# Modulation tiles loaded ahead of their use, eight scaled tiles per boundary, and head sums as single float32 products

## The chip, the cores and the metric

The kernel runs on one core of a Trainium2 chip. The time is device microseconds (us) of one execution. Three executions of the kernel before took 2766.11, 2750.26 and 2754.33 us; the time before is their median, 2754.33 us.

## What is computed

One sequence of 256 tokens with 2048 channels goes through two layers, all in float32. The first layer mixes time by an RWKV-7 recurrence (32 heads of 64 channels), the second by attention over chunks of 64 tokens that reads one shared pair of keys and values. Each has a squared-ReLU MLP of 8192 hidden channels behind it. Ahead of every block the residual stream is normed and modulated, and its gate comes from the same modulation. Cut to what the change touches:

```python
def rms_norm(x, g):
    return x * rsqrt(mean(x * x, axis=-1) + RMS_EPS) * g
def modulate(h, shift, scale):
    return h * (1 + scale) + shift

for layer in range(2):
    sh1, sc1, gt1, sh2, sc2, gt2 = split(c @ w_ada[layer] + b_ada[layer], 6)
    if layer == 1:
        sh_kv, sc_kv = split(c @ w_ada_kv + b_ada_kv, 2)
        h_kv = modulate(rms_norm(x, g_kv), sh_kv, sc_kv)
        kp, vp = h_kv @ w_k_shared, h_kv @ w_v_shared
    h = modulate(rms_norm(x, g_mix[layer]), sh1, sc1)
    y = rwkv7_time_mix(h, ...) if layer == 0 else chunk_band_attention(h, kp, vp, ...)
    x = x + gt1 * y                     # y ends in a 2048x2048 product, "out projection"
    h = modulate(rms_norm(x, g_mlp[layer]), sh2, sc2)
    x = x + gt2 * (square(relu(h @ w_up[layer])) @ w_down[layer])
return rms_norm(x, g_final)

# inside rwkv7_time_mix, per head: three sums over the head's 64 channels
kk = kk / max(sqrt(sum(kk * kk)), 1e-12)
y = (y - mean) * rsqrt(mean((y - mean)**2) + GN_EPS) * ln_w + ln_b
y = y + sum(r * k * r_k) * v
```

## The kernel before

**Matrices.** Channels lie on the 128 partitions and tokens on the free axis, so the stream x is 16 tiles of 128x256. A weight tile gives 128 output channels: 128x2048 numbers, loaded in two halves of 512 KB by SyncE (SP, `raw`, L364) into six buffers. TensorE multiplies in the rounded format fp32r, so every operand is a rounded part H and a rest L: ScalarE (ACT) casts a half to wH (L374), VectorE (DVE) subtracts to get wL (L377), with three buffers of each. A product over 2048 channels is 16 "k-tiles". `proj2` (L408, L409) does wH with both parts of the activation side by side (512 columns) and wL with its H part (256 columns). `proj` (L397 to L399) does the three products of 258 columns each; two extra columns carry the shift.

**Boundaries.** A new block needs the norm of all 16 tiles of x. So that TensorE need not wait for it, the first RAW = 4 weight tiles of the block multiply "scaled" tiles, x times a gain, with no norm in them (`scaled`, L527 on ACT and L528 on DVE); the factor 1/rms and the shift are put on the product (`late_norm`, L542 and L543). Meanwhile the 16 normed tiles are made (`normed_tile`, L518 to L520), four behind each of these four tiles, for the rest of the block with `proj2`. The sum of squares ss is added up by POOL, the last tile by DVE (L495, L496); `rstd` (L500 to L510) is a product with ones over ss (m, L501), four DVE steps and two ACT steps. An out projection adds to x at L885, a down projection of an MLP at L947. There are four such boundaries: first out projection to first MLP, first MLP to the shared keys, second out projection to second MLP, and the end.

**Modulation.** w_ada has 384 tiles of 128x1024 that TensorE doesn't multiply as matrices: DVE multiplies a tile by the scalars of c and adds it to a running tile acc (L435 for the first, L437 for the others), and after 16 tiles TensorE sums acc over partitions (L449) and DVE adds the bias (L453). One tile is a "modulation step", which both loads and adds. 102 steps lie in the RWKV stage (244 to 754 us), where they share the six raw buffers of the weights; later stages have buffers of their own ("rada", 5, 5, 3 and 5 of them). `ada(n)` does n steps; `ada_tick` in the MLP one, and two at every third call; `ada_need` does all that are missing of a part. The RWKV stage works on 16 pairs of heads.

**Head sums.** Each of the three sums is a product with a block matrix of ones. `parts` (L112 to L117) has ACT make the rounded part, ACT again the exact value (for squares) and POOL the difference; `head_sums` (L122) multiplies both parts.

**Order.** Each engine runs its instructions in the order in which they stand in its queue. That order is made ahead of time from the order of the Python calls, with moves by a scheduler; `issue_after` ties a piece to stand behind a given instruction. A load stands in SP's queue and waits there for its buffer; what stands behind it waits too.

## Time and profile before

| | |
|---|---|
| median of three executions | 2754.33 us |
| profiled execution | 2753.33 us, of which the span on the engines is 2751.5 us |
| mean granted TensorE clock | 0.987 of full |
| read from HBM | 656.72 MB, 239 GB/s over the span |

The profile is of one execution. A line of it names the engine, the line of the kernel's text, the operation and its tiles as output <- inputs, and then times; "x" with a number counts instructions. Up to about 244 us the first projections of the RWKV stage run, to 754 its pairs of heads, to 832 the first out projection, to 1560 the first MLP, to 1905 keys, values, queries and attention, to 2000 the second out projection, and then the second MLP.

### The profile page before, as it was taken

How to read it: one execution, taken by the hardware profiler on the slowest of the kernel's cores; microseconds unless marked ns; L12 is line 12 of the kernel's file. 1: busy time of each engine (PE TensorE's matmuls, PEld its weight loads, DVE VectorE, ACT ScalarE, POOL GpSimd, SP SyncE). 2: the span in 40 equal slices, each digit the busy share in tenths (PEclk: the TensorE clock that was granted, in tenths of full speed). 3: DMA queues.
4: the chain of work that ended last, by engine and by line, in shares of the span. 5: the costliest groups of instructions: out<-in, count | busy, mean ns of one | idle time of the engine just before them, and what ended most of it. 6: DMA issues, size and time to landing. Idle time of an engine off the chain costs nothing.

```text
span 2751.5 us, 58214 instructions
## 1 busy us (share of the span) xinstructions
PE 2651.1 (96%) x23594; PEld 2231.8 (81%) x23594; DVE 2078.0 (76%) x3033; ACT 1368.1 (50%) x2501; POOL 288.3 (10%) x416
## 2 busy tenths in 40 slices
PE   6998999999989999999999899999999999999997
PEld 3677777777878888888888888877888888888886
DVE  4568788878798888888889995799896555556555
ACT  2345555556346446445355454465455354463554
POOL 0003443443210000000000100000100000000002
PEclk9999999999999999999999999999999999999999
DMA  9886556555687988888888777878776555555553
GB/s 307 270 277 194 169 179 192 181 173 162 202 322 267 319 311 312 306 305 307 310 309 307 269 258 238 291 261 282 269 248 211 187 189 186 189 185 189 186 190 124
DMA packets 217389, 662.62 MB, mean 241 GB/s; under 512 B 21408, under 2 KB 68896, under 8 KB 217120
## 3 DMA queue, kind: packets, MB, share of 16 engines
q1 hardware_dynamic: 215056, 656.36, 71.2%
q8 instruction: 185, 3.03, 0.4%
q10 hardware_dynamic: 2064, 2.54, 0.3%
q14 instruction: 84, 0.69, 0.1%
HBM read 656.72 MB, written 2.10 MB: 239 GB/s over the span
## 4 chain that ended last, share of the span: by engine, by line
PE 84%; DVE 7%; DMA 3%; issue 3%; POOL 1%; ACT 1%; DVEq 0%; SPq 0%; ACTq 0%; POOLq 0%
PE pj L408 45%; PE pj L409 22%; DVE wL L377 2%; PE iv L105 2%; DMA rada<-w_ada 1%; PE gr L99 1%; PE m L655 1%; DVE acc L437 1%; PE ms L99 1%; PE o L397 1%; POOL sL L117 1%; PE chn L278 1%; PE py L320 1%; PE chn L285 1%; PE v L751 0%
## 5 line engine op out<-in xcount | busy, mean ns | idle before, releaser
L408 PE MATMUL pj<-aHL,wH 128*128 128x512 f32 x3520 | 1283.6, 405 | 6.1 <-DVE x L885 2.0
L377 DVE TENSOR_TENSOR wL<-raw,wH 128x1024 fp32r<-128x1024 f32 x772 | 946.2, 1226 | 371.4 <-ACT wH L374 368.5
L374 ACT CAST wH<-raw 128x1024 fp32r<-128x1024 f32 x772 | 805.8, 1045 | 768.3 <-PE pj L408 667.4
L409 PE MATMUL pj<-aHL,wL 128*128 128x256 f32 x3520 | 994.6, 283 | 6.4 <-DVE wL L377 6.4
L408 PEld LDWEIGHTS pj<-aHL,wH 128*128 128x128 f32 x3520 | 667.7, 190 | 168.0 <-issue 12.4
L408 PE MATMUL pj<-hHL,wH 128*128 128x512 f32 x2048 | 717.5, 396 | 0.0
L409 PEld LDWEIGHTS pj<-aHL,wL 128*128 128x128 f32 x3520 | 667.6, 190 | 10.6 <-DVE wL L377 8.7
L409 PE MATMUL pj<-hHL,wL 128*128 128x256 f32 x2048 | 571.0, 279 | 0.0
L408 PEld LDWEIGHTS pj<-hHL,wH 128*128 128x128 f32 x2048 | 384.3, 188 | 91.8
L409 PEld LDWEIGHTS pj<-hHL,wL 128*128 128x128 f32 x2048 | 385.9, 188 | 0.2
L437 DVE SCALAR_TENSOR_TENSOR acc<-rada,ct,acc 128x1024 f32<-128x1024 f32 x265 | 339.0, 1279 | 39.8 <-DMA rada<-w_ada 33.7
L496 POOL TENSOR_TENSOR ss<-ss,sq 128x256 f32<-128x256 f32 x56 | 53.1, 948 | 1592.3 <-ACT sq L495 1592.1
L947 DVE SCALAR_TENSOR_TENSOR x<-pj,mod,x 128x256 f32<-128x256 f32 x256 | 123.3, 482 | 59.6 <-PE pj L409 56.3
L437 DVE SCALAR_TENSOR_TENSOR acc<-raw,ct,acc 128x1024 f32<-128x1024 f32 x95 | 127.1, 1338 | 0.2
L919 ACT ACTIVATE t<-t 128x256 f32<-128x256 f32 x120 | 50.1, 417 | 136.2 <-DVE t L897 136.2
L399 PE MATMUL pj<-aHL,wL 128*128 128x258 f32 x192 | 57.5, 300 | 7.1 <-DVE wL L377 7.1
L655 PE MATMUL m<-rawa,crep 128*32 128x256 f32 x512 | 47.3, 448 | 16.7 <-DMA rawa<-w_ada 16.2
L397 PE MATMUL pj<-aHL,wH 128*128 128x258 f32 x192 | 57.2, 298 | 1.4 <-ACT wH L374 0.9
L398 PE MATMUL pj<-aHL,wH 128*128 128x258 f32 x192 | 57.1, 298 | 0.0
L921 ACT ACTIVATE t<-t 128x256 f32<-128x256 f32 x128 | 53.4, 417 | 3.3
L920 ACT ACTIVATE hHL<-t 128x256 fp32r<-128x256 f32 x128 | 52.9, 414 | 3.9 <-DVE t L543 2.8
L922 DVE TENSOR_TENSOR hHL<-t,hHL 128x256 fp32r<-128x256 f32 x128 | 53.7, 419 | 1.3 <-ACT t L921 0.8
(248 smaller groups left out, 2867.7 us busy)
## 6 DMA issues: line engine op xcount, KB each, us to landing
raw<-w_up SPq DMA_DIRECT2D x256, 512.0 KB, 4.5
raw<-w_down SPq DMA_DIRECT2D x256, 512.0 KB, 4.4
rada<-w_ada SPq DMA_DIRECT2D x218, 512.0 KB, 6.2
raw<-w_ada SPq DMA_DIRECT2D x102, 512.0 KB, 4.1
rawa<-w_ada SPq DMA_DIRECT2D x64, 512.0 KB, 6.7
rada<-w_ada_kv SPq DMA_DIRECT2D x64, 512.0 KB, 6.5
raw<-w_k SPq DMA_DIRECT2D x32, 512.0 KB, 4.2
raw<-w_r SPq DMA_DIRECT2D x32, 512.0 KB, 4.7
```

The lines of the kernel that those rows point to most:

```text
L99: self.b.nc.tensor.matmul(o(c)[K], lhsT(c)[K], rhs(c)[K], start=True, stop=True)
L105: self.b.nc.tensor.matmul(o[QS[K], c, :], lhsT[QS[R], c, :], rhs[QS[R], c, :], start=True, stop=True, tile_position=(H * R, H * K))
L374: nc.scalar.copy(Hf, raw)
L377: eng.tensor_tensor(out=Lf, in0=raw, in1=Hf, op=ALU.subtract)
L397: nc.tensor.matmul(ps, H[:, i, :], a(kt)[:, 0, :], start=(first and kt == 0), stop=False)
L398: nc.tensor.matmul(ps, H[:, i, :], a(kt)[:, 1, :], start=False, stop=False)
L399: ins = nc.tensor.matmul(ps, L[:, i, :], a(kt)[:, 0, :], start=False, stop=(last and kt == KT - 1))
L408: nc.tensor.matmul(ps, H[:, i, :], a(kt), start=(kt == 0), stop=False)
L409: ins = nc.tensor.matmul(ps[:, 0, :], L[:, i, :], a(kt)[:, 0, :], start=False, stop=(kt == KT - 1))
L437: nc.vector.scalar_tensor_tensor(out=acc, in0=raw, scalar=ck, in1=acc, op0=ALU.mult, op1=ALU.add)
L655: nc.tensor.matmul(ps[g:g + 32, part, :W], crep[:, kt, :], raw[:, i, :], start=(part == 1 and kt < 4), stop=(part == 0 and kt >= KT - 4), ...
L947: nc.vector.scalar_tensor_tensor(out=x, in0=ps[:, i, :], scalar=self.mods[(layer, 5)][:, n:n + 1], in1=x, op0=ALU.mult, op1=ALU.add)
```

## The change

It has four parts.

1. **Modulation as a queue.** Loading and adding are apart: `ada_load` issues a load, `ada_step` adds the oldest loaded tile, `ada_fill` loads ahead until all but one of the stage's buffers are taken. `ada_fill` runs after each `ada(n)` and at the start of a block; `ada_drain` only adds what is loaded and issues no load.
2. **Where steps stand.** In the out projections tiles 10 to 15 only drain one each, tiles 8 and 9 have a step, and tiles 0 to 7 have one in the second projection alone. The last seven tiles of an MLP only drain. `ada_tick` does one and two steps in turn, and starts at tile RAW - 2 of the MLP. A tile of V has two steps (one before), a tile of Q one, or two for every third (two before). The parts that the query needs are awaited behind the scaled tiles of K, not ahead of them.
3. **RAW is 8** in place of 4, so two normed tiles stand behind each of eight scaled tiles. `rstd` is issued after the first eight k-tiles of the first scaled tile.
4. **Head sums** are one product of the float32 tile with a float32 matrix of ones; `parts` is gone, and a square is one ACT instruction.

```diff
-RAW = 4
+RAW = 8
...
-    def head_sums(self, ps, parts):
-        for i, t in enumerate(parts):
-            self.b.nc.tensor.matmul(ps, self.b.bones, t, start=(i == 0), stop=(i == 1))
+    def head_sums(self, ps, t):
+        self.b.nc.tensor.matmul(ps, self.b.cst("bones"), t, start=True, stop=True)
+    def square(self, src, scale=1.0):
+        t = self.s("sq", 2)
+        self.b.nc.scalar.activation(t, src, AF.Square, scale=scale)
+        return t
...
-        sq = self.parts(AF.Square, k, vec("k_k", j))
+        sq = self.square(k, vec("k_k", j))
...
             yield
+            self.ada_drain(n)
             self.ada_pool = None
...
+    def ada_load(self):
+        tile_ = next(self.adas, None)
+        if tile_ is not None:
+            key, half, kt = tile_
+            w, n_ = self.ada_src(*key)[0], HK * P
+            raw = self.raw(w[kt * P:(kt + 1) * P, half * n_:(half + 1) * n_], ada=True)
+            self.ada_q.append((key, half, kt, raw))
+        return tile_ is not None
+    def ada_step(self):
         nc = self.nc
+        if not (self.ada_q or self.ada_load()):
+            return
+        key, half, kt, raw = self.ada_q.popleft()
...
+    def ada_fill(self):
+        while self.ada_pool and len(self.ada_q) < self.ada_pool[1] - 1 and self.ada_load():
+            pass
+    def ada_drain(self, n):
+        for _ in range(min(n, len(self.ada_q))):
+            self.ada_step()
...
     def ada(self, n=1):
         for _ in range(n):
-            next(self.adas, None)
+            self.ada_step()
+        self.ada_fill()
...
                 self.ss_add(x, n, nc.vector if n == KT - 1 else None)
-                self.ada()
+                if n < KT - 6 and (n >= 8 or not begun):
+                    self.ada()
+                elif n >= KT - 6:
+                    self.ada_drain(1)
...
-        rstd, hl, nxt = self.rstd(), self.new_hl(), None
+        rstd, hl, nxt = None, self.new_hl(), None
+        self.ada_fill()
...
             if q == 0 and f < RAW:
-                self.proj(ps[:, :TE], w, lambda kt: scaled[:, kt])
+                ins = self.proj(ps[:, :TE], w, lambda kt: scaled[:, kt], (0, HK))
+                if rstd is None:
+                    with tc.issue_after(ins):
+                        rstd = self.rstd()
+                self.proj(ps[:, :TE], w, lambda kt: scaled[:, kt], (HK, KT))
...
-            if q or f >= RAW:
+            if q or f >= RAW - 2:
                 self.ada_tick(layer)
...
-                self.ada_tick(layer)
+                if q == NQ - 1 and n >= KT - 7:
+                    self.ada_drain(1)
+                else:
+                    self.ada_tick(layer)
...
-        self.nticks = getattr(self, "nticks", 0) + 1
-        self.ada(2 if self.nticks % 3 == 0 else 1)
+        self.nticks = getattr(self, "nticks", 0) + 10
+        self.ada(self.nticks // 20 + 1)
+        self.nticks %= 20
...
-        self.ada_need((1, 1), (1, 0))
         for j in range(RAW):
...
+        self.ada_need((1, 1), (1, 0))
         gain, hq = self.gain("g_mix1", (1, 1)), self.new_hl()
...
-            projected(d["w_v_shared"][j], hkv, t, 1, (none, none, turn))
+            projected(d["w_v_shared"][j], hkv, t, 2, (none, none, turn))
...
-                projected(d["w_q"][j], hq, qs[j], 2, ...
+                projected(d["w_q"][j], hq, qs[j], 1 + (j % 3 == 0), ...
```

The first place is DVE's queue in the first out projection, before and then after. acc is a modulation step, x the update of the stream, aHL a scaled tile, wL the rest of a weight half.

```order
L437 SCALAR_TENSOR_TENSOR acc<-rada,ct,acc 128x1024
L885 SCALAR_TENSOR_TENSOR x<-o,mod_2_72,x 128x256
L437 SCALAR_TENSOR_TENSOR acc<-rada,ct,acc 128x1024
L528 SCALAR_TENSOR_TENSOR aHL<-x,gain_g_mlp_11405,aHL 128x256
L885 SCALAR_TENSOR_TENSOR x<-o,mod_2_72,x 128x256
L437 SCALAR_TENSOR_TENSOR acc<-rada,ct,acc 128x1024
L528 SCALAR_TENSOR_TENSOR aHL<-x,gain_g_mlp_11405,aHL 128x256
L437 SCALAR_TENSOR_TENSOR acc<-rada,ct,acc 128x1024
L377 TENSOR_TENSOR wL<-raw,wH 128x1024
```
```order
L894 SCALAR_TENSOR_TENSOR x<-o,mod_2_72,x 128x256 x2
L370 TENSOR_TENSOR wL<-raw,wH 128x1024
L539 SCALAR_TENSOR_TENSOR aHL<-x,gain_g_mlp_11163,aHL 128x256
L370 TENSOR_TENSOR wL<-raw,wH 128x1024
L539 SCALAR_TENSOR_TENSOR aHL<-x,gain_g_mlp_11163,aHL 128x256
L370 TENSOR_TENSOR wL<-raw,wH 128x1024
L894 SCALAR_TENSOR_TENSOR x<-o,mod_2_72,x 128x256 x2
L370 TENSOR_TENSOR wL<-raw,wH 128x1024
L539 SCALAR_TENSOR_TENSOR aHL<-x,gain_g_mlp_11163,aHL 128x256 x2
L370 TENSOR_TENSOR wL<-raw,wH 128x1024
L443 SCALAR_TENSOR_TENSOR acc<-rada,ct,acc 128x1024
```

Both pieces begin after the first wL of a whole half (128x1024) and the two scaled tiles behind it. Before, four modulation steps stand ahead of the next wL; after, two x updates do, and the first modulation step follows the sixth.

The second place is DVE's queue where the first MLP ends and the keys begin (rv is the first DVE step of `rstd`).

```order
L437 SCALAR_TENSOR_TENSOR acc<-rada,ct,acc 128x1024
L377 TENSOR_TENSOR wL<-raw,wH 128x1024
L437 SCALAR_TENSOR_TENSOR acc<-rada,ct,acc 128x1024
L947 SCALAR_TENSOR_TENSOR x<-pj,mod_5_75,x 128x256
L377 TENSOR_TENSOR wL<-raw,wH 128x1024
L947 SCALAR_TENSOR_TENSOR x<-pj,mod_5_75,x 128x256
L528 SCALAR_TENSOR_TENSOR aHL<-x,gain_g_kv,aHL 128x256
L496 TENSOR_TENSOR ss<-ss,sq 128x256
L437 SCALAR_TENSOR_TENSOR acc<-rada,ct,acc 128x1024
L503 TENSOR_SCALAR rv<-m 128x256
```
```order
L443 SCALAR_TENSOR_TENSOR acc<-rada,ct,acc 128x1024
L539 SCALAR_TENSOR_TENSOR aHL<-x,gain_g_kv,aHL 128x256
L370 TENSOR_TENSOR wL<-raw,wH 128x1024
L965 SCALAR_TENSOR_TENSOR x<-pj,mod_5_75,x 128x256 x2
L370 TENSOR_TENSOR wL<-raw,wH 128x1024
L539 SCALAR_TENSOR_TENSOR aHL<-x,gain_g_kv,aHL 128x256
L507 TENSOR_TENSOR ss<-ss,sq 128x256
L443 SCALAR_TENSOR_TENSOR acc<-rada,ct,acc 128x1024 x2
L514 TENSOR_SCALAR rv<-m 128x256
```

The step that stood right ahead of the last x updates is gone from there; the one left stands further ahead and uses a tile that was loaded earlier. Two steps, before one, stand between ss and rv.

The third place is SP's queue in the V projection.

```order
L364 DMA raw<-w_v_shared 128x1024 x16
L364 DMA rada<-w_ada 128x1024
L364 DMA raw<-w_v_shared 128x1024
L364 DMA rada<-w_ada 128x1024 x2
L364 DMA raw<-w_v_shared 128x1024 x2
L364 DMA rada<-w_ada 128x1024
```
```order
L357 DMA raw<-w_v_shared 128x1024 x16
L357 DMA rada<-w_ada 128x1024 x2
L357 DMA raw<-w_v_shared 128x1024
L357 DMA rada<-w_ada 128x1024 x3
L357 DMA raw<-w_v_shared 128x1024 x2
L357 DMA rada<-w_ada 128x1024 x3
```

In both, sixteen half tiles of V are asked for with no modulation tile among them; behind these, up to three modulation tiles stand between two weight halves, before one or two.

More of the change, by code (lines that the diff above doesn't have):

```diff
@@ L1 @@
 import math
+from collections import deque
 from contextlib import ExitStack, contextmanager, nullcontext
@@ L309, in late @@
         var, pg = pyt[:, 1, :], pyt[:, 1, :]
-        sq = self.parts(AF.Square, py)
+        sq = self.square(py)
         yield
```

73 lines of the change are left out of this document (31 added, 42 removed).

## The prediction

> **What bounds the kernel now.** I read the page's engine totals first, then a table of busy time by stage, then what TensorE (PE) waited for, then the timelines of VectorE (DVE) and PE around the longest waits.
>
> ```profile
> PE 2651.1 (96%) x23594; PEld 2231.8 (81%) x23594; DVE 2078.0 (76%) x3033; ACT 1368.1 (50%) x2501; POOL 288.3 (10%) x416
> ```
> ```profile
> 244.00:754.00 510.00, 496.82 (x9428) 390.03 (x9427) 411.74 (x755) 265.77 (x738) 204.19 (x268) 0.99 0.58 181
> 754.00:832.00 78.00, 68.91 (x488) 61.66 (x487) 71.91 (x87) 38.77 (x61) 11.71 (x14) 0.96 0.87 309
> 832.00:860.00 28.00, 24.62 (x177) 23.36 (x176) 26.60 (x56) 17.88 (x32) 0.00 (x0) 0.94 0.58 200
> 860.00:1545.00 685.00, 684.84 (x4512) 597.29 (x4511) 581.46 (x673) 345.30 (x507) 11.18 (x11) 1.00 0.88 309
> 1545.00:1600.00 55.00, 44.55 (x361) 41.33 (x360) 48.49 (x80) 26.70 (x43) 3.70 (x13) 0.94 0.69 230
> 1895.00:2000.00 105.00, 96.09 (x571) 80.41 (x570) 92.04 (x120) 45.69 (x73) 11.34 (x13) 0.93 0.78 265
> 2000.00:2040.00 40.00, 34.88 (x298) 33.06 (x298) 35.22 (x67) 22.77 (x39) 1.00 (x1) 0.91 0.67 222
> 2040.00:2735.00 695.00, 695.00 (x4020) 605.31 (x4019) 416.38 (x509) 351.10 (x517) 15.26 (x14) 1.00 0.58 189
> ```
>
> The columns of the table are the stretch and its length, busy time of PE, weight load, DVE, ACT and POOL, PE's granted clock, and DMA share and GB/s. PE bounds the kernel: inside the first MLP (860 to 1545) it is busy 684.84 of 685 us, inside the second 695 of 695, both at full clock. Nothing is to be had there. The time that can be had lies at the boundaries: PE is idle 9.1 us in 754:832 (first output projection), 3.4 in 832:860 (start of the first MLP), 10.5 in 1545:1600 (into attention), 8.9 in 1895:2000 (into and through the second output projection) and 5.1 in 2000:2040 (start of the second MLP), 37.0 us in all. In the same five rows the clock is below 1: (1 - clock) times length gives 3.1 + 1.7 + 3.3 + 7.4 + 3.6 = 19.1 us, of which the share that falls on idle time costs nothing.
>
> ```profile
> PE m L501 <- DVE ss L496: 8.9, 2, 7.6
> PE pj L399 <- DVE wL L377: 7.1, 5, 2.1
> PE o L399 <- DVE wL L377: 7.1, 2, 6.3
> PE pj L409 <- DVE wL L377: 6.4, 6, 3.2
> PE pj L408 <- DVE x L885: 2.0, 1, 2.0
> ```
>
> These are PE's longest waits between 755 and 2060 (total, times, longest). All end with DVE: the rest of a weight half (wL), the sum of squares (ss), an update of x. Why DVE is late there shows in its own timeline, first in the first output projection, then at the end of the first MLP:
>
> ```profile
> 766.12 1.27 DVE L437 SCALAR_TENSOR_TENSOR acc<-rada,ct,acc 128x1024 f32<-128x1024 f32 x1
> 767.32 1.21 DVE L377 TENSOR_TENSOR wL<-raw,wH 128x1024 fp32r<-128x1024 f32 x1
> ```
> ```profile
> 1561.98 1.28 DVE L437 SCALAR_TENSOR_TENSOR acc<-rada,ct,acc 128x1024 f32<-128x1024 f32 x1 [2.21 <-DMA rada<-w_ada]
> 1563.19 0.48 DVE L947 SCALAR_TENSOR_TENSOR x<-pj,mod,x 128x256 f32<-128x256 f32 x1
> ...
> 1566.17 0.42 DVE L496 TENSOR_TENSOR ss<-ss,sq 128x256 f32<-128x256 f32 x1
> ```
>
> Modulation steps (acc, 1.27 us each) stand in DVE's queue ahead of the work that PE waits for, and one of them sits 2.21 us on its own load with the last x update behind it. PE's 6.3 us wait ends with the wL of 767.32, its 7.6 us wait with the ss of 1566.17.
>
> **The change part by part.** The counts below are of DVE's order before and after.
>
> *Steps 1 to 5, the boundaries.* Sixteen modulation steps stand between the first x update and the first MLP before, ten after, and none of them before the sixth x update; 22 stand in the second output projection before, 10 after; the last ones of each stage use tiles loaded earlier. In the first six tiles of each MLP none stand. With eight scaled tiles the 16 normed tiles are spread over about 45 us of PE work in place of 22. One tile then asks DVE for two wL, a late norm, the hidden split and two normed tiles, by the start-to-start times of these rows 4.8 us, less than PE's 5.8 (step 7).
>
> - 754:832: the 6.3 us wait ended with a wL behind four acc (5.1 us, the last is the row of 766.12); in the new order the same wL has two x updates ahead of it. I take 7.5 of 9.1 us of idle.
> - 832:860: no acc stood there; half the normed work per tile removes the waits for wL. 3.0 of 3.4.
> ```profile
> 1580.00:1600.00 20.00, 17.19 (x184) 15.92 (x183) 19.96 (x40) 12.04 (x21) 1.10 (x10) 1.00 0.55 185
> ```
>
> - 1545:1600: no load wait ahead of the last x updates. But three acc still stand between ss and the first late norm. 9.0 of 10.5; next late is ss itself, a chain of x update, square, add, that nothing shortens.
> - 1895:2000: four acc still stand ahead of the fifth wL, the attention's tail has short waits of its own, so I take only 4.0 of 8.9.
> - 2000:2040: as in the first MLP, 4.5 of 5.1.
>
> The clock comes on top:
>
> ```profile
> 764.00:767.00 3.00, 0.00 (x0) 0.00 (x0) 3.00 (x4) 0.81 (x2) 0.78 (x1) 0.69 1.03 407
> 767.00:770.00 3.00, 1.42 (x6) 1.42 (x7) 3.00 (x4) 0.00 (x0) 0.00 (x0) 0.50 1.04 406
> ```
> ```profile
> 844.00:847.00 3.00, 3.00 (x16) 3.00 (x15) 3.00 (x9) 2.26 (x5) 0.00 (x0) 0.50 0.72 236
> ```
>
> After a boundary wait PE runs at 0.50 for some 3 us, which costs half of that. I take 1.4, 1.6, 1.6, 3.0 and 2.0 us (of the 3.1, 1.7, 3.3, 7.4 and 3.6 above, less what falls on idle time; in the fourth, whose wait I let stand in part, less than half). The half clock at 844 followed waits of which none was over 2.1 us (the longest of the L399 row).
>
> The Trainium skill, page "TensorE: Matmul & The Clock Gate", section "What's actually happening", has the clock halve only after an idle window of about 3.4 us and return after as long a busy one. By it the second, fourth and fifth boundary would carry no clock part, and the forecast would be some 6.6 us later; the row at 844 shows the half clock after shorter waits, so the row decides.
>
> Wait and clock give 8.9, 4.6, 10.6, 7.0 and 6.5: **37.6 us less**. The lower end is 2.8 us (only what PE idles after 1580, behind normed work: 20 - 17.19), the upper 37.0 + 13.6 = 51.
>
> *Step 6, head sums.* 48 sums (three for each of 16 pairs) lose one of two products, three of five ScalarE operations, and the subtract on POOL, which is the last to finish. The rows are of the chain of waits, where PE's steps show start-to-start times (start, length, what):
>
> ```profile
> 421.86 3.44 POOL sL L117 x2
> ...
> 426.44 0.23 PE ms L122 x2
> ...
> 431.51 0.63 PE ms L132 x2
> 432.14 0.43 PE ms L133 x2
> 437.16 0.44 PE ms L122 x2
> ```
>
> The pair of rounded products takes 0.23 us, or 0.44 behind another kind of matmul. One float32 product over 256 columns shows as two records: 0.43 (L133), or 0.63 where it comes first (L132). So each sum costs 0 to 0.40 more, and I take 0.20, by like against like: +9.6 us in a stretch (244:754) where PE is busy 496.8 of 510. What PE waited for POOL's subtract between 244 and 754:
>
> ```profile
> PE py L122 <- POOL sL L117: 5.8, 4, 2.2
> ...
> PE ms L122 <- POOL sL L117: 0.9, 2, 0.5
> ```
>
> Against the 9.6 stand these 5.8 + 0.9 = 6.7 us; ScalarE's one square comes 3.4 us earlier than POOL's result did in the rows above, so these go. Net **+2.9**, between 0 - 6.7 = -6.7 and +19.2.
>
> *Step 7, twelve more tiles with 258 columns.* From a view of one line's instructions, with their starts:
>
> ```profile
> L397 PE MATMUL pj<-aHL,wH x27: 277/282/382, 1570.5 to 1579.9; 128*128 128x258 f32 x27
> ```
>
> Its 26 gaps take 9.4 us: three products of 258 columns take 0.362 us a k-tile, a tile 5.8. The wide form takes two products a k-tile: 4020 in the 695 us of the last MLP's row, 0.346, a tile 5.5. Twelve tiles of 16 k-tiles: 192 x 0.016 = **+3.0** (+2 to +4 by the rounded starts).
>
> *Step 8, what the steps do where they go.* The first MLP takes 185 steps, before 170; in the V projection five tiles carry three steps each.
>
> ```profile
> L377 DVE TENSOR_TENSOR wL<-raw,wH 128x1024 fp32r<-128x1024 f32 x772 | 946.2, 1226 | 371.4 <-ACT wH L374 368.5
> ...
> L437 DVE SCALAR_TENSOR_TENSOR acc<-rada,ct,acc 128x1024 f32<-128x1024 f32 x265 | 339.0, 1279 | 39.8 <-DMA rada<-w_ada 33.7
> ```
>
> A V tile with three steps needs 2 x 1.23 + 3 x 1.28 + 0.42 = 6.7 us of DVE against PE's 5.5: five times 1.2 is 6, part of which the three weight buffers hide. Their loads, five of 0.524 MB in 5.5 us, ask 477 GB/s, but eight tiles before them ask almost none, and six buffers wait full. On the SP queue each such load also waits for its buffer with the next weight behind it. I take **+4.0**, between -2 (more loads ahead, fewer of the 33.7 us of DVE's waits) and +19: at 309 GB/s, the mean of the first MLP's row, 2.62 MB take 8.5 us and 2.1 MB 6.8; five tiles are 3.0 us late each, and three 1.3.
>
> The Trainium skill, page "DMA: Bandwidth & Descriptors", section "Where 436 GB/s comes from", has loads from HBM bound at about 358 GB/s for a core. By it the five tiles would need 7.3 us each, 9 us more in all, and the forecast would be 5 us later. The stretch 764 to 770 moved 406 and 407 GB/s, so the measurement decides.
>
> **The sum.** -37.6 + 2.9 + 3.0 + 4.0 = -27.7. The profiled execution took 2753.3 us (span 2751.5); that is 1 us under the median of the three runs. 2753.3 - 27.7 = 2725.6, **2726**.
>
> **Rivals.** A difference of 0.5% (13.8 us) is about what a measurement of this kernel can tell from no change.
>
> - *The wait is replaced at the two attention boundaries.* For it: acc still stand ahead of the fifth wL and behind ss. Against it: their loads are issued earlier. Then the third term is only its 2.8, the fourth nothing: -22.8 + 9.9 = -12.9, 2740.
> - *The steps are not the cause.* PE would wait for wL and ss anyway, through ScalarE's casts or the clock. For it: at 832 waits stood with no acc near. Against it: the two DVE timelines. Only steps 6 to 8 remain, +9.9: 2763, no measurable change.
> - *The denser stretches become bound by loads* (slower). The first MLP then moves (256 + 185) x 0.524 = 231 MB in about 719 us, 322 GB/s; it decides against the kernel where less than that can be kept up. At the 309 GB/s of its row it would take 748, 29 us more, and V the 19 us of step 8: -27.7 - 4 + 29 + 19 = +16, 2769. Against it: 407 GB/s was reached, and PE never waited in 860:1545.
> - *More is gained:* every boundary wait and its clock loss go, 51 us, and the head sums cost nothing: under 2702.
>
> **Chances.** Forecast (2702 to 2736) 0.55; first rival (to 2751) 0.20; steps not the cause 0.09; denser stretches 0.08; more gained 0.08. The range, 2702 to 2751, leaves out the last three. It takes in the bounds of step 6 (-9.6 to +16.3 around its value) and of step 8 (-6 to +15), one at a time. Faster by over 0.5%, that is under 2740.5: 0.55 + 0.08 and half of the first rival, 0.73; slower 0.08; within, 0.19.
>
> **What would show it.** Right: the waits for wL and ss at the five boundaries fall from 37 us to under 10, and their clock is near 1; no line for POOL in the pair stretch, which stays within 5 us of its length; the inner MLP stretches stay full. Wrong: PE idle inside 860:1545 or in V with DMA at its ceiling (third rival); 10 us or more in the pair stretch (step 6 at its upper end); a new wait for the fifth wL near 1910 (first rival); or a wait for ss of several us at 1560.

## The result

The changed kernel took 2719.8 us (median of five runs, 2715.85 to 2725.59); the kernel before, beside it, 2754.24 us. The ratio is 0.9871, 95% interval 0.9847 to 0.9895: 1.3% faster, some 35 us. The forecast was 2726 us, in a range of 2702 to 2751.

The engine totals of the changed kernel's profile (2719.8 us, span 2718.0):

```profile
PE 2649.5 (97%) x23786; PEld 2237.3 (82%) x23786; DVE 2072.1 (76%) x3045; ACT 1348.1 (50%) x2432; POOL 227.4 (8%) x368
```

In sum PE is as busy as before (2651.1), and what went is time in which it waited; the parts of the busy time moved, though: less of it is at half clock, more of it goes into the head sums and the first MLP (see the part on the prediction). For the comparison the span is cut at the same events in every kernel, in order: the pairs (first `pj` product to the last `py<-tg`), the rest of the first out projection (to the first scaled `pj`), the up tiles of the first MLP's first block (to its first down product), the rest of that MLP (to the first scaled product of K), K (to the first transpose of V), V (to the first S), Q and attention (to the last po), the second out projection, the up tiles of the second MLP's first block, and the rest of that MLP. Here are the rows of the changed kernel in the table by stage (stretch, length, busy PE, weight load, DVE, ACT, POOL, clock, DMA share, GB/s):

```profile
217.10:747.10 530.00, 525.74 (x9571) 411.49 (x9572) 424.24 (x794) 270.29 (x732) 146.58 (x226) 1.00 0.57 183
747.10:813.40 66.30, 63.19 (x383) 55.90 (x382) 60.28 (x73) 34.75 (x55) 12.33 (x14) 0.97 0.86 294
813.40:906.20 92.80, 92.48 (x708) 86.32 (x707) 84.29 (x128) 57.18 (x96) 0.24 (x1) 1.00 0.79 268
906.20:1553.40 647.20, 642.17 (x4290) 557.89 (x4289) 557.00 (x643) 315.00 (x451) 12.49 (x14) 0.99 0.86 317
1553.40:1660.20 106.80, 103.25 (x700) 95.93 (x699) 92.28 (x146) 55.09 (x82) 1.38 (x11) 0.98 0.76 252
1660.20:1760.00 99.80, 97.68 (x676) 84.50 (x674) 78.69 (x81) 43.46 (x64) 0.00 (x0) 0.98 0.86 301
1760.00:1898.70 138.70, 138.07 (x985) 106.81 (x984) 124.23 (x279) 82.23 (x222) 6.50 (x54) 1.00 0.78 259
1898.70:1981.60 82.90, 81.77 (x467) 71.09 (x466) 74.59 (x87) 42.58 (x61) 12.71 (x14) 1.00 0.80 276
1981.60:2074.30 92.70, 92.50 (x708) 86.35 (x707) 83.95 (x127) 57.17 (x96) 0.00 (x0) 1.00 0.71 243
```

The same view of both profiles, length in us, with PE's idle time (length less busy) in brackets:

| stretch | before | changed | difference | term of the forecast |
|---|---|---|---|---|
| pairs | 533.5 (13.2) | 530.0 (4.3) | -3.5 | +2.9 |
| first out projection | 71.7 (7.8) | 66.3 (3.1) | -5.4 | -8.9 |
| first MLP, first up tiles | 98.8 (4.6) | 92.8 (0.3) | -6.0 | -4.6 |
| rest of the first MLP | 633.8 (0.2) | 647.2 (5.0) | **+13.4** | part of +4.0 |
| K | 114.5 (10.5) | 106.8 (3.6) | -7.7 | -10.6 |
| V | 97.1 (1.9) | 99.8 (2.1) | +2.7 | part of +4.0 |
| Q and attention | 138.5 (2.5) | 138.7 (0.6) | +0.2 | 0 |
| second out projection | 99.0 (7.2) | 82.9 (1.1) | **-16.1** | -7.0 |
| second MLP, first up tiles | 100.0 (4.6) | 92.7 (0.2) | -7.3 | -6.5 |
| rest of the second MLP | 628.9 (0.0) | 628.2 (0.0) | -0.7 | 0 |

What lies ahead of the pairs (219.7 and 217.1 us) and behind the last product (16.0 and 15.5) gives the rest. The 258-column tiles (+3.0) are spread over three stretches. So the boundaries gave 42.5 us, the first MLP took 13 back. The stretches hold nearly the same work in every kernel, not quite: the sum of half a modulation part over partitions (64 small products, 0.7 us) falls in one stretch or the next, and PE does some 5 k-tiles (1.9 us) of the second out projection ahead of the last po in the changed kernel that it did behind it before. So Q, attention and the second out projection are best taken together: 237.5 us before, 221.6 in the changed kernel. PE's waits between 755 and 2060 in the changed kernel:

```profile
PE pj L402 <- DVE wL L370: 5.0, 4, 2.1
PE m L512 <- DVE ss L507: 3.2, 3, 2.7
PE pj L401 <- ACT wH L367: 2.8, 1, 2.8
```

The waits for wL and ss are what is left of the five rows of before. The third is new: PE waits for a cast, so for a weight load. It ends at 921 us, 15 us behind the first down product of the first MLP.

### The profile page after: what moved, and what is told of

It reads as the page before. It is cut to its first block, busy times and chain, and to the rows that moved or that the text cites. A ratio compares the mean times of both kernels' runs of the same rounds, so it can differ in the third digit from the quotient of the medians.

```text
span 2718.0 us, 58600 instructions
## 1 busy us (share of the span) xinstructions
PE 2649.5 (97%) x23786; PEld 2237.3 (82%) x23786; DVE 2072.1 (76%) x3045; ACT 1348.1 (50%) x2432; POOL 227.4 (8%) x368
## 4 chain that ended last, share of the span: by engine, by line
PE 88%; DVE 4%; DMA 3%; issue 3%; ACT 1%; POOL 0%; DVEq 0%; SPq 0%; ACTq 0%; POOLq 0%
PE pj L401 44%; PE pj L402 22%; PE iv L106 2%; DVE wL L370 2%; PE pj L391 1%; PE pj L392 1%; PE pj L390 1%; PE gr L100 1%; DVE acc L443 1%; PE m L666 1%; PE ms L100 1%; PE o L390 1%; DMA rada<-w_ada 1%; PE chn L270 1%; PE ms L110 1%
## 5 line engine op out<-in xcount | busy, mean ns | idle before, releaser
L401 PE MATMUL pj<-aHL,wH 128*128 128x512 f32 x3328 | 1217.6, 406 | 2.0 <-DVE x L894 1.1
L402 PE MATMUL pj<-aHL,wL 128*128 128x256 f32 x3328 | 939.9, 282 | 4.3 <-DVE wL L370 4.3
L401 PEld LDWEIGHTS pj<-aHL,wH 128*128 128x128 f32 x3328 | 629.4, 189 | 155.7 <-issue 11.8
L402 PEld LDWEIGHTS pj<-aHL,wL 128*128 128x128 f32 x3328 | 629.9, 189 | 9.0 <-DVE wL L370 5.7
L391 PE MATMUL pj<-aHL,wH 128*128 128x258 f32 x384 | 109.6, 286 | 0.0
L390 PE MATMUL pj<-aHL,wH 128*128 128x258 f32 x384 | 109.6, 285 | 0.0
L392 PE MATMUL pj<-aHL,wL 128*128 128x258 f32 x384 | 108.7, 283 | 0.8 <-DVE wL L370 0.8
L937 ACT ACTIVATE t<-t 128x256 f32<-128x256 f32 x112 | 46.8, 418 | 111.4 <-DVE t L909 111.3
L392 PEld LDWEIGHTS pj<-aHL,wL 128*128 128x128 f32 x384 | 74.0, 193 | 1.1 <-DVE wL L370 1.1
L391 PEld LDWEIGHTS pj<-aHL,wH 128*128 128x128 f32 x384 | 73.4, 191 | 0.1
L390 PEld LDWEIGHTS pj<-aHL,wH 128*128 128x128 f32 x384 | 73.0, 190 | 0.2
```

The costliest lines, as they stand in the source:

```text
L390: nc.tensor.matmul(ps, H[:, i, :], a(kt)[:, 0, :], start=(first and kt == 0), stop=False)
L391: nc.tensor.matmul(ps, H[:, i, :], a(kt)[:, 1, :], start=False, stop=False)
L392: ins = nc.tensor.matmul(ps, L[:, i, :], a(kt)[:, 0, :], start=False, stop=(last and kt == KT - 1))
L401: nc.tensor.matmul(ps, H[:, i, :], a(kt), start=(kt == 0), stop=False)
L402: ins = nc.tensor.matmul(ps[:, 0, :], L[:, i, :], a(kt)[:, 0, :], start=False, stop=(kt == KT - 1))
```

## The experiments

All profiles cut in the same way, lengths in us, and the median of each run's own time. The kernel before had medians of 2754 to 2758 beside them, so medians of different groups of runs differ by some 4 us on that account alone; the ratios to before in the text don't have this.

| run | pairs | out 1 | up 1 | rest 1 | K | V | Q, att. | out 2 | up 2 | median |
|---|---|---|---|---|---|---|---|---|---|---|
| before | 533.5 | 71.7 | 98.8 | 633.8 | 114.5 | 97.1 | 138.5 | 99.0 | 100.0 | 2754.2 |
| changed | 530.0 | 66.3 | 92.8 | 647.2 | 106.8 | 99.8 | 138.7 | 82.9 | 92.7 | 2719.8 |
| after_again | 529.1 | 64.9 | 92.8 | 644.0 | 107.0 | 97.9 | 138.6 | 83.3 | 92.7 | 2718.6 |
| sums_old | 537.1 | 66.4 | 92.8 | 645.2 | 107.8 | 97.4 | 138.6 | 83.0 | 92.7 | 2729.4 |
| sums_only | 528.6 | 71.7 | 97.5 | 636.9 | 112.3 | 96.7 | 140.5 | 95.2 | 99.0 | 2750.4 |
| raw4 | 529.9 | 66.4 | 95.2 | 639.4 | 114.3 | 102.3 | 133.9 | 83.7 | 95.9 | 2730.4 |
| raw8_only | 536.1 | 72.0 | 93.6 | 637.9 | 106.3 | 95.9 | 137.9 | 106.4 | 92.4 | 2749.3 |
| ahead_off | 531.3 | 62.2 | 95.5 | 643.7 | 103.3 | 97.4 | 141.8 | 82.6 | 92.7 | 2719.3 |
| place_old | 530.8 | 81.0 | 95.8 | 639.5 | 102.9 | 100.1 | 134.3 | 84.6 | 91.8 | 2725.5 |
| vq_old | 532.8 | 65.0 | 92.8 | 648.4 | 106.5 | 96.4 | 140.3 | 92.9 | 92.7 | 2730.6 |
| q_pool | 530.0 | 68.7 | 92.7 | 640.7 | 109.4 | 98.3 | 138.7 | 83.4 | 92.6 | 2724.6 |
| skip4 | 528.9 | 66.4 | 92.8 | 635.9 | 102.6 | 97.1 | 138.0 | 87.7 | 92.7 | 2713.9 |
| skip4_rate | 530.4 | 64.9 | 92.8 | 638.3 | 108.2 | 97.8 | 138.6 | 83.0 | 92.7 | 2715.4 |
| pairs7 | 537.9 | 66.6 | 92.7 | 638.2 | 102.5 | 96.9 | 141.2 | 86.6 | 94.7 | 2716.7 |

A repeat shows how far such stretches are to be trusted:

> The changed kernel once more, unedited, as the measure for the two runs beside it and for how far stretches with the same instructions differ between executions. 2716 to 2726; the stall near the first down product of the first MLP (PE idle 5.0 us, 647.2 us to K) comes again if it is the kernel's and not that execution's.

The stall came again (3.1 us idle in "rest 1", 5.0 the first time), and most stretches agree within 1 us; "rest 1", V and the first out projection differ by 3, 2 and 1.4 us. The stretch ahead of the pairs, the same in all kernels, took 216.4 to 221.4 us.

### Head sums: sums_old and sums_only

```diff
+    def parts(self, func, src, scale=1.0): ...   # as before
-    def head_sums(self, ps, t):
-        self.b.nc.tensor.matmul(ps, self.b.cst("bones"), t, start=True, stop=True)
+    def head_sums(self, ps, parts):
+        for i, t in enumerate(parts):
+            self.b.nc.tensor.matmul(ps, self.b.bones, t, start=(i == 0), stop=(i == 1))
```

That is sums_old, the changed kernel with this part undone; sums_only is the reverse edit on the kernel before.

> The changed kernel with the old head sums (rounded part, exact value, POOL's difference, two products). Theory A (the head sums themselves made the pair stretch shorter, 533.6 to 530.0 us, because the waits for POOL weighed more than the longer product): the pair stretch is back at 533 to 534, PE idles some 9 us more in it, the whole is 3 to 4 us slower than the changed kernel. Theory B (the prediction's: a single float32 product costs 0.2 us more per sum, and something else shortened the stretch): the pair stretch gets 2 to 4 us shorter, 526 to 528. Stretches behind it stay within 1 us in both.

> The kernel before with the new head sums alone. Theory A (the single products save what PE waited for POOL, and more than they cost): the pair stretch is 530 in place of 533.6 us, 3 to 4 us faster in all, 2751. Theory B (the shorter pair stretch needs the queue of modulation tiles too): it stays at 533 to 536.

Both show theory A, with more than it asked for. Undone, the pairs take 537.1 us, 7.1 more, and the kernel's ratio to before is 0.9906 (0.9891 to 0.9921) in place of 0.9871; done alone, the pairs take 528.6, 4.9 fewer (ratio 0.9976, 0.9963 to 0.9989). The rows of the kernel before and of sums_only:

```profile
219.70:753.20 533.50, 520.32 (x9570) 410.33 (x9571) 432.66 (x794) 284.49 (x781) 207.98 (x274) 0.99 0.58 182
```
```profile
217.30:745.90 528.60, 525.44 (x9571) 411.26 (x9572) 423.89 (x794) 270.03 (x732) 146.54 (x226) 1.00 0.58 184
```

PE is busy 5.1 us more and idle 10.0 less (3.2 in place of 13.2). The clocks of the rows, 0.99 and 1.00, belong to the reckoning: before, 6.8 of the busy us ran at half clock, which lost 3.4, and in sums_only none did. So the 48 sums cost 5.1 + 3.4 = 8.5 us, 0.18 each, and sums_old gives the same (5.05 lost at half clock, 522.16 busy against 525.74: 8.6 us). That is near the 0.20 of the forecast; what it missed is that 10.0 us of waits went and not the 6.7 of POOL's subtract, and the half clock behind them. What else went shows in PE's waits of sums_only in this stretch, where the wait of `iv` for DVE's tt, 4.2 us in the same view of the kernel before, is 0.4:

```profile
PE iv L105 <- DVE zs L291: 2.1, 3, 0.7
PE pj L399 <- DVE v L714: 0.9, 1, 0.9
PE iv L105 <- DVE tt L228: 0.4, 1, 0.4
```

Why tt came earlier was not tried apart.

### Eight scaled tiles: raw4 and raw8_only

```diff
-RAW = 8
+RAW = 4
...
-            if q or f >= RAW - 2:
+            if q or f >= 6:
```

This is raw4; raw8_only sets RAW = 8 in the kernel before.

> The changed kernel with four scaled tiles per boundary in place of eight (modulation steps start at the same tile of the MLP). Theory A (the normed tiles spread over twice the time take away PE's waits behind normed work, 832:860 and 2000:2040 before): the stretches from the first scaled to the first down product, 92.8 and 92.7 us in the changed kernel, get some 4 to 6 us longer each, the one of K some 2 us; 10 to 12 us slower in all. Theory B (the modulation steps alone were the cause): these stretches get about 1 us shorter each by the faster form of product, 3 us faster in all.

> The kernel before with eight scaled tiles per boundary alone (modulation steps in the MLP then start at tile 8, as its own rule has it). Theory A (spreading the normed tiles takes away waits, whatever the modulation does): first scaled to first down product falls from 98.8 and 100.0 to 94 and 95, and K's stretch (114.5) by 2 to 4; 10 us faster. Theory B (it helps only where the modulation steps are out of the way too): these fall by under 2 us each.

Theory A holds in both, with sizes of its own. Alone, eight tiles take 8.2 us from K and 5.2 and 7.6 from the two MLPs' up tiles, which are then as short as in the changed kernel; yet the kernel gets only 0.9969 of before (0.9959 to 0.9978), since the second out projection, with 31 modulation steps in place of 21, goes from 99.0 to 106.4 us and the rest of the first MLP from 633.8 to 637.9. Taken from the changed kernel, K is back at 114.3, the up tiles lose 2.4 and 3.2 us, and the whole loses 10.6 us by the medians (ratio 0.9904, 0.9888 to 0.9921, in place of 0.9871). So K gets shorter only with the scaled tiles. In raw4 the wait for ss at the start of K is short too, 2.9 us, but waits for wL (3.8 us) and 10.2 us at half clock follow it. The stall behind the first down product isn't there in raw4 (PE busy 639.4 of 639.4).

### Load ahead and place: ahead_off and place_old

```diff
     def ada(self, n=1):
         for _ in range(n):
             self.ada_step()
-        self.ada_fill()
```

ahead_off also drops the two other calls of `ada_fill`. place_old puts the steps back where they stood at the ends of stages:

```diff
-                if n < KT - 6 and (n >= 8 or not begun):
-                    self.ada()
-                elif n >= KT - 6:
-                    self.ada_drain(1)
+                self.ada()
...
-                if q == NQ - 1 and n >= KT - 7:
-                    self.ada_drain(1)
-                else:
-                    self.ada_tick(layer)
+                self.ada_tick(layer)
```

> The changed kernel where a modulation tile is loaded only when its step is due (no load ahead, nothing left to drain), all steps else where they stand. Theory A (the places of the steps give the gain, the load ahead little): the boundaries stay within 3 us of the changed kernel's. Theory B (load ahead gives a good part): DVE waits for modulation loads again (7.6 us in the changed kernel, 39.8 before), the boundaries lose 5 us or more. On the first MLP, which got 13.3 us longer from its first down product to K (633.9 to 647.2): if loads issued ahead hold up the weights in SP's queue, this stretch gets 5 us or more shorter without them; if only the number of steps in it counts, it stays.

> The changed kernel with modulation steps again behind every tile of the out projections and behind the last down tiles, loads ahead kept. Theory A (the places of the steps give most of the gain at the boundaries): the first out projection to the scaled tiles (66.3 us in the changed kernel) gets 3 to 5 us longer, the second (83.0) 8 to 14, K (106.8) 2 to 5; 12 to 20 us slower. Theory B (the load ahead was what counted): under 5 us slower in these three together.

Loading ahead is worth nothing here: 2719.3 us without it, 2719.8 with it, and the boundaries are as short or shorter (the first MLP's up tiles lose 2.7 us). DVE does wait for more loads in all, but PE doesn't feel it:

```profile
L443 DVE SCALAR_TENSOR_TENSOR acc<-rada,ct,acc 128x1024 f32<-128x1024 f32 x265 | 339.2, 1280 | 19.9 <-DMA rada<-w_ada 18.9
```

The stretch with the stall has 643.7 us and 4.2 of idle, as in the repeat of the changed kernel (644.0 and 3.1), so the early calls don't make it. SyncE runs ahead by itself: the loads of the stall below each go out within 0.03 us of the end of the step that frees their buffer, so there is little that a call ahead of time can gain.

Of place_old only one stretch went the way of theory A, the first out projection: 81.0 us, 14.7 more than in the changed kernel, and three times what was asked for. It has 21 steps there, the kernel before 16 (71.7 us), the changed one 10 (66.3). PE's longest wait in it, 6.2 us, is for acc itself: the product that sums a modulation part stands in PE's own queue. The second out projection took 1.7 more (8 to 14 expected), K 3.9 less; the 12.5 us of the three together lie in theory A's range only by that one stretch. By the count of acc only 8 steps were left for the second out projection, since others were done earlier; the place there was not what mattered.

### How many steps are left: vq_old

```diff
-            projected(d["w_v_shared"][j], hkv, t, 2, (none, none, turn))
+            projected(d["w_v_shared"][j], hkv, t, 1, (none, none, turn))
...
-                projected(d["w_q"][j], hq, qs[j], 1 + (j % 3 == 0), ...
+                projected(d["w_q"][j], hq, qs[j], 2, ...
```

> The changed kernel with one modulation step per tile of V and two per tile of Q, as before. Theory A (the second out projection got 16 us shorter, 99.0 to 83.0, because fewer steps are left for it and DVE comes out of the Q stretch without a backlog): it gets 5 to 12 us longer again, the stretch from the first S product to the last po stays at 138 or gets longer, V gets 2 us shorter; 5 to 10 us slower in all. Theory B (it is the drained last tiles and the loads ahead that did it): the second out projection stays within 2 us of 83, V gets 2 us shorter, the whole is not slower.

Theory A: 92.9 us in place of 82.9, and a ratio to before of 0.9901 (0.9884 to 0.9917) in place of 0.9871. The length follows the count of steps. Taken over Q, attention and the second out projection together, where every profile has the same products, the steps and the us are:

| steps | us |
|---|---|
| 30 | 217.6 (raw4), 218.9 (place_old) |
| 34 | 221.6 to 222.1 (changed, its repeat, sums_old, q_pool, skip4_rate) |
| 38 to 40 | 227.8 (pairs7), 224.4 (ahead_off), 225.7 (skip4) |
| 48 | 233.2 (vq_old) |
| 49 | 237.5 (before), 235.7 (sums_only) |
| 62 | 244.3 (raw8_only) |

A straight line through the fourteen has 0.86 us a step, two thirds of the 1.28 that one takes. The two ends in the second out projection alone, from the line view of DVE, first the changed kernel, then raw8_only, and the rows of before and raw8_only in the table by stage:

```profile
L443 DVE SCALAR_TENSOR_TENSOR acc<-rada,ct,acc 128x1024 f32<-128x1024 f32 x11 | 14.5, 1319 | 1.9 <-DMA rada<-w_ada 1.9
```
```profile
L437 DVE SCALAR_TENSOR_TENSOR acc<-rada,ct,acc 128x1024 f32<-128x1024 f32 x29 | 38.0, 1311 | 3.3 <-DMA rada<-w_ada 3.3
```
```profile
1907.60:2006.60 99.00, 91.77 (x607) 78.60 (x604) 85.63 (x103) 44.43 (x64) 12.34 (x14) 0.93 0.79 266
1901.00:2007.40 106.40, 93.44 (x619) 79.31 (x618) 97.38 (x113) 44.69 (x64) 14.24 (x14) 0.95 0.87 299
```

(Two more steps of raw8_only are the first of their part, a different operation.) In raw8_only DVE is the busier engine, 97.4 of 106.4 us against PE's 93.4; before it was not, 85.6 of 99.0 against 91.8. So the stretch as a whole is not bound by DVE. What a step costs is seen on PE: over the two stretches PE waits 9.8 us before, 7.7 in vq_old and 1.8 in the changed kernel, and loses 6.4, 4.8 and 0 us at half clock behind such waits.

### The stall: q_pool, skip4, skip4_rate, pairs7

The load queue of SyncE and the modulation steps of DVE in the changed kernel, just ahead of the stall (timeline: start, length, what; a load's length is how long its group took to issue):

```profile
899.64 1.27 SPq L357 DMA_DIRECT2D raw<-w_down  x1
901.89 3.00 SPq L357 DMA_DIRECT2D rada<-w_ada_kv  x2
904.98 0.38 SPq L357 DMA_DIRECT2D raw<-w_down  x1
907.43 4.63 SPq L357 DMA_DIRECT2D rada<-w_ada_kv  x3
912.11 0.90 SPq L357 DMA_DIRECT2D raw<-w_down  x2
```
```profile
906.12 1.28 DVE L443 SCALAR_TENSOR_TENSOR acc<-rada,ct,acc 128x1024 f32<-128x1024 f32 x1
...
909.31 0.75 DVE L441 TENSOR_SCALAR acc<-rada,ct 128x1024 f32<-128x1024 f32 x1
910.09 1.29 DVE L443 SCALAR_TENSOR_TENSOR acc<-rada,ct,acc 128x1024 f32<-128x1024 f32 x1
```

The three loads of the group at 907.43 go out one by one as DVE ends a step and frees a buffer: the first behind the step of 906.12 (906.12 + 1.28 is 907.40), the next two 2.65 and 3.97 us later, behind the steps of 909.31 and 910.09. Meanwhile from 899.64 to 912.11 two weight halves are issued, where a tile needs two every 5.5 us. What follows, by 4 us:

```profile
908.00:912.00 4.00, 4.00 (x56) 3.57 (x48) 3.67 (x6) 1.50 (x4) 0.00 (x0) 1.00 0.89 315
912.00:916.00 4.00, 4.00 (x25) 3.51 (x24) 3.17 (x4) 0.80 (x1) 0.00 (x0) 1.00 0.72 220
916.00:920.00 4.00, 2.33 (x14) 1.80 (x12) 3.96 (x5) 0.00 (x0) 0.00 (x0) 1.00 0.95 343
920.00:924.00 4.00, 2.06 (x6) 1.56 (x7) 2.99 (x5) 2.14 (x3) 0.00 (x0) 0.70 1.03 412
924.00:930.00 6.00, 6.00 (x25) 5.15 (x24) 3.86 (x4) 2.04 (x2) 0.00 (x0) 0.63 1.02 409
```

The memory has room before the stall (220 GB/s at 912:916) and is full only behind it; then PE runs at 0.63 to 0.70. Four runs test this.

q_pool loads the modulation tiles of the MLPs, up to the last block of down tiles, from GpSimd's queue:

```diff
-        self.nc.sync.dma_start(out=t, in_=src)
+        (self.ada_eng if ada and self.ada_pool else self.nc.sync).dma_start(out=t, in_=src)
...
+        self.ada_eng = nc.gpsimd     # mlp, at its start; nc.sync from its last block of down tiles on
```

> The changed kernel where the modulation tiles of the first MLP (up to its last block of down products) are loaded from GpSimd's queue in place of SyncE's. Theory A (a modulation load that waits for its buffer holds up the weight loads behind it in SyncE's queue; from 899 to 912 us only two weight halves were issued): the stretch from the first down product to K gets 7 to 12 us shorter, 635 to 640, and PE idles under 1 us in it. Theory B (the loads are bound by what the memory gives, 409 to 412 GB/s in the stall): it stays at 645 to 648. Other stretches stay within 2 us.

PE is idle 0.5 us and the stretch has 640.7, 0.7 above theory A's range: the weights no longer stand behind the modulation loads. As a kernel it gains nothing (ratio to before 0.9873; K has 2.6 us more, and the first out projection, ahead of the edited loads, 2.4).

skip4 leaves DVE's and SyncE's queues clear at that place; skip4_rate makes the steps up later, so that by the order of the instructions every stage has as many as in the changed kernel:

```diff
-                else:
+                elif q or n >= 4:
                     self.ada_tick(layer)
...
-        self.nticks = getattr(self, "nticks", 0) + 10
+        self.nticks = getattr(self, "nticks", 0) + 11
```

(The last two lines are skip4_rate's alone.)

> The changed kernel with no modulation step behind the first four down tiles of every MLP block's first... that is of the first block only. Theory A (steps that pile up at the change from up to down tiles, with their loads ahead of the weights in SyncE's queue, make the stall): PE idles under 1 us between the first down product and K, and that stretch is 638 to 641 in place of 647.2; as the steps left out there have to be done by K at the latest, 2 to 4 us of it come back near K; 3 to 6 us faster in all. Theory B (the stall comes from the up tiles ahead of it): it stays, 645 or more.

> The kernel of the run before last (no modulation steps behind the first four down tiles of an MLP's first block) with the steps left out there made up over the rest of the MLP (1.55 steps a tick on average, not 1.5), so that by the order of the instructions the first MLP has 185 steps, attention 61 and the second out projection 10, all as in the changed kernel. Theory A (the place of those steps made the stall, not their number): the first MLP from its first down product to K stays at 636 to 640 with under 2 us of idle time, and the second out projection, which had 87.7 us with 15 steps, is back at 83; 8 us faster than the changed kernel, about 2710. Theory B (fewer steps in the MLP removed the stall): 644 to 648 with 3 to 5 us idle again, 2717 to 2720.

> The changed kernel with seven modulation steps in a pair's time in place of six, 119 in the pair stretch and not 102, so that 17 fewer are left for the first MLP and what follows. Theory A (VectorE has room there, busy 412 of 510 us before): the pair stretch gets under 3 us longer (530.0), the stall in the first MLP is gone (638 to 641), V and the second out projection stay; 4 to 8 us faster in all, 2713 to 2716. Theory B (17 steps of 1.3 us push VectorE's work for the pairs, which is waited for): the pair stretch gets 8 us or more longer, and nothing is gained.

pairs7 is `ADA_SLOTS = (1, 3, 5, 7, 9, 11, 14)` in place of `(1, 3, 6, 9, 11, 14)`. In all three the stall is gone: PE is idle 1.3 us in that stretch in skip4 (theory A asked for under 1), 0.1 in skip4_rate and 0.2 in pairs7. The row of skip4_rate:

```profile
904.80:1543.10 638.30, 638.17 (x4290) 555.43 (x4289) 557.08 (x642) 314.01 (x451) 11.96 (x13) 1.00 0.89 321
```

With the same 185 steps in the MLP PE is idle 0.1 us: their place made the stall, not their number. The place alone doesn't always make it: raw4 and place_old have steps behind the same down tiles and no idle time (639.4 and 639.5 us); what decides is open. The memory gives 321 GB/s over the whole stretch without holding PE up. In the kernel's time the stall doesn't show: skip4_rate, expected at about 2710 us, has 2715.4 and a ratio to before of 0.9872 (0.9853 to 0.9890), that of the changed kernel. The steps that skip4 leaves out were expected back near K, which got shorter (102.6 us); they came back in Q and the second out projection (40 steps in place of 34, 4.1 us). pairs7 has its price where theory B put it: the pairs take 537.9 us, and nothing is gained. skip4 has the lowest median, 2713.9 us, a ratio to before of 0.9856 (0.9835 to 0.9876), beside 0.9883 (0.9863 to 0.9904) of the changed kernel, measured together with it. It is clearly ahead of the kernel before; ahead of the changed one by its median only, as the intervals overlap.

## Why the prediction was right, and where its terms were not

The time, its sign and the main mechanism came out: modulation steps and normed work on DVE held PE up at the boundaries, and with their removal PE's idle time in the five boundary stretches fell from 34.7 to 8.3 us. That the time came within 6 us is in part luck, as single terms were further off than the sum, in both directions.

The forecast split each boundary into idle time and half clock. The profiles give both: idle time is a stretch's length less PE's busy time, and the half clock costs half of the busy time that ran at a granted clock of 0.50. What is left is PE's own work. In us, booked and measured (the second out projection with Q and attention, as the border between them moved; the forecast's windows differ from these stretches by some us):

| boundary | idle, booked | idle, measured | half clock, booked | half clock, measured | PE's work, measured |
|---|---|---|---|---|---|
| first out projection | -7.5 | -4.7 | -1.4 | -0.1 | -0.6 |
| first MLP, first up tiles | -3.0 | -4.3 | -1.6 | -1.7 | 0.0 |
| K | -9.0 | -6.9 | -1.6 | -0.3 | -0.5 |
| second out projection | -4.0 | -8.0 | -3.0 | -6.4 | -1.5 |
| second MLP, first up tiles | -4.5 | -4.4 | -2.0 | -3.3 | +0.4 |
| sum (unrounded) | -28.0 | -28.3 | -9.6 | -11.9 | -2.1 |

The two sums are right; the division among the boundaries is not.

- **First boundary** (-8.9, measured -5.4). The wait of 6.3 us went, as said. A new one of 2.1 us came, for a later wL, and half clock behind it. Modulation steps make it again, further on than the forecast looked: in the changed kernel three of them stand ahead of the wL of 777.22, with which the wait ends.

```profile
772.36 1.27 DVE L443 SCALAR_TENSOR_TENSOR acc<-rada,ct,acc 128x1024 f32<-128x1024 f32 x1
773.55 0.47 DVE L894 SCALAR_TENSOR_TENSOR x<-pj,mod,x 128x256 f32<-128x256 f32 x1
773.95 1.27 DVE L443 SCALAR_TENSOR_TENSOR acc<-rada,ct,acc 128x1024 f32<-128x1024 f32 x1
775.14 0.96 DVE L539 SCALAR_TENSOR_TENSOR aHL<-x,gain_g_mlp,aHL 128x256 fp32r<-128x256 f32 x1
776.02 1.27 DVE L443 SCALAR_TENSOR_TENSOR acc<-rada,ct,acc 128x1024 f32<-128x1024 f32 x1
777.22 1.22 DVE L370 TENSOR_TENSOR wL<-raw,wH 128x1024 fp32r<-128x1024 f32 x1
```

- **First up tiles of both MLPs** (-4.6 and -6.5, measured -6.0 and -7.3). Right; raw4 and raw8_only confirm the normed tiles as the cause.
- **K** (-10.6, measured -7.7). The size is near, the reason was at best half of it. The step said that nothing waits for a load ahead of the last x updates; the wait for ss did fall, from 7.6 to 2.7 us. But raw8_only, with all loads as before, has K at 106.3 and the same short wait (2.5 us), and raw4, with the new places and four scaled tiles, has the short wait and K at 114.3. So the scaled tiles are needed for the gain. Which shift of the order shortens the wait for ss is open.
- **Second out projection** (-7.0, measured -16.1, or -15.9 with Q and attention). This is the step that failed by most: the wait that I let stand. I took 4.0 of 8.9 us of idle time and 3.0 of 7.4 of half clock, as four steps stand ahead of the fifth wL; but in the changed kernel PE has no wait for a wL there at all (the last four steps ahead of the wL of 1900.53 ran from 1892.81 to 1900.28, and its one wait is of 1.1 us, for x). Nearly the whole 16.3 us of that row went. vq_old shows why: the steps that V takes over are missing here. In step 8 of the forecast I booked these only as a cost.
- **Head sums** (+2.9, measured -3.5 to -7.1). The sign was wrong. The price of the product was about right (0.18 us a sum, 0.20 booked); what was mis-sized are the waits, 8.9 to 10.7 us in the three comparisons in place of 6.7, and the half clock behind them, 3.4 to 5.1 us, was not booked at all.
- **Denser stretches** (+4.0, measured +13.4 in the MLP and +2.7 in V, at the upper end of -2 to +19). One of the forecast's own signs of being wrong was seen, PE idle inside the MLP, but the third rival is not its cause: 321 GB/s went through without a wait. It was the sentence on SyncE's queue, "each such load also waits for its buffer with the next weight behind it", that deserved the price. Of the 13.4 us, 4.9 are idle time, 3.0 the half clock behind it and 1.4 two more sums of modulation parts (704 small products in place of 576). The 4.1 that are left are about what the pace of PE does between executions (last section): raw8_only and sums_only, with the products of before and no idle time, have 637.9 and 636.9 us in place of 633.8. Of V's 2.7 us, 1.7 are half clock, which the repeat doesn't have.
- **258-column tiles** (+3.0). The 0.346 us a k-tile of the wide form counts 64 small products of a modulation sum (0.7 us) among the 4020. In the first up tiles of the changed kernel the medians from start to start are 0.120 + 0.122 + 0.119 = 0.361 us for the three products and 0.234 + 0.118 = 0.352 for the two, so twelve tiles cost 192 x 0.009 = 1.7 us.

Against the forecast, the boundaries with their wider tiles gave 7.7 us more and the head sums 6.4, the denser stretches cost 12.1 more, and 3.8 us are of stretches that no term is about (ahead of the pairs, the rest of the second MLP, the end). That these cancel to 6 us is luck.

## What to carry to other kernels

Side work that may run at any time should be counted against the spare time of its engine in each stage: where another engine waits for it, a step moved out was worth two thirds of its length here, in waits and in the half clock behind them; so count the steps, beside the waits that they stand right ahead of. A load that waits for a buffer holds up every load behind it in its queue (two weight halves in 12.5 us here), so slow side loads need a queue of their own or a place where nothing urgent follows. An engine that only subtracts one rounded part from another may be the last to finish in a chain: look at what waits for it, and at what its removal brings forward, before the product that it saves is priced.

## What the runs showed of the hardware

PE's pace differs between executions at a granted clock of 1.00. The rest of the second MLP has the same instructions in the changed kernel and in q_pool, and PE is never idle:

```profile
2074.30:2702.50 628.20, 628.20 (x3648) 548.12 (x3647) 364.65 (x449) 311.47 (x448) 15.52 (x14) 1.00 0.56 182
```
```profile
2071.90:2703.30 631.40, 631.40 (x3648) 549.04 (x3647) 364.56 (x449) 311.41 (x448) 15.46 (x14) 1.00 0.56 181
```

That is 0.5%, 3.2 us, so differences of that size between two profiles say little. These are two kernels with the same work there; the same kernel's two profiles, the changed one and its repeat, have 628.2 and 629.8.

The half clock doesn't follow from the length of a wait alone. The same wait for wL in the first out projection, 2.1 us long in both, was followed by 3 us at half clock in the first profile of the changed kernel and by none in its repeat:

```profile
778.50:781.50 3.00, 3.00 (x10) 2.62 (x11) 3.00 (x5) 0.81 (x2) 0.15 (x1) 0.50 0.78 252
```
```profile
781.50:784.50 3.00, 3.00 (x17) 2.64 (x18) 3.00 (x5) 1.00 (x3) 0.14 (x1) 1.00 0.79 262
```

The fourteen profiles show more. In each, all changes of the granted clock lie on a grid of 3.413 us, to within 3 ns, so the half clock lasts 3.41 us or a multiple of it. From the pairs to the end of the second MLP, a cell of this grid in which PE was idle for 1.84 us or more was always followed by one at half clock; behind a cell at full clock with less than 1.24 us of idle time there never was one; in between both occur. In the first profile 1.90 us of the wait fell into one cell (774.8 to 778.2), in the repeat 1.40.

The Trainium skill, page "TensorE: Matmul & The Clock Gate", section "What's actually happening", says that activity is judged over a free-running window of about 3.4 us; that one wait can cost 1.4 us or nothing (66.3 and 64.9 us for the stretch) agrees with this, but the half clock did come after a wait shorter than the idle window that it names.
